# Second mixer of a two-layer encoder: two gated projections placed between pairs of the attention, scores as two products over 64 rows, one gate by exp

## The chip, the cores and the metric

The kernel runs on one core of a Trainium2 chip. Its time is the device time of one execution in microseconds (us); lower is better. TensorE (PE) multiplies matrices, VectorE (DVE) and ScalarE (ACT) work elementwise, GpSimd (POOL) helps and issues some of the DMAs, and SyncE (SP) issues the weight loads.

## The reference

512 tokens (two sequences of 256) of width 1024 pass through two layers; each is a mixer, a layernorm, a convolutional feed-forward part (FFN) and another layernorm. The first layer's mixer is a neighbourhood attention and is left as it was. The change is in the second layer's mixer:

```python
def odd_mixer(x, cos, sin, w_in, q_norm_g, w_uq, kv_norm_g, w_ukv,
              conv_w, conv_b, conv_ln_g, conv_ln_b, w_out):
    h = x @ w_in
    c_q, c_kv, k_r, glu_a, glu_g = split(h)            # 256, 128, 32, 512, 512 columns
    c = latent_attention(c_q, c_kv, k_r, ...)
    d = glu_a * jax.nn.sigmoid(glu_g)
    d = jax.nn.silu(layernorm(dwconv(d, conv_w, conv_b), conv_ln_g, conv_ln_b))
    return jnp.concatenate([c, d], axis=-1) @ w_out

def latent_attention(c_q, c_kv, k_rope_in, ...):       # 8 heads
    q_nope, q_rope = split(rmsnorm(c_q) @ w_uq)        # 64 and 32 per head
    k_nope, v = split(rmsnorm(c_kv) @ w_ukv)           # 64 and 64 per head
    q_rope, k_rope = apply_rope(q_rope), apply_rope(k_rope_in)   # k_rope is shared by the heads
    s = (q_nope . k_nope + q_rope . k_rope) * 96 ** -0.5
    return softmax(s) @ v
```

The depthwise convolution `dwconv` has 31 taps over 512 channels.

## The kernel before

Everything stays on chip as features by tokens (128 partitions x 512 tokens). A float32 matrix is split into two parts, hi and lo (ACT makes `whi`, DVE `wlo`), and a product is three matmuls of 128x512. The scores and their product with V stay in plain float32, where the trace records each matmul twice: `s` x4 in a row of the trace are two products.

The second mixer works on these pieces:

- `glu(i)`, i = 0 to 3: the gated projection of 128 channels, 48 matmuls into two banks of PSUM (tile `glu`). ACT takes the sigmoid of the second bank (L541, tile `sig`), DVE multiplies it with the first (L545, tile `dpad`). The convolution of the channels follows: 20 taps on DVE into a PSUM bank (`cacc`, L706), 9 as products on ACT (`pr`, L710, a ring of two halves) that POOL adds up (`acc`, L711). At the end DVE adds both (L712). `accps` and `acc2` hold the two sums.
- `cproj`, `chain`: the projection to q, k and rope inputs, the rms norm, the rotation of the rope part of k, and transposes back (tiles `craw`, `cT`, `krT`).
- `kvproj`, `qproj`: V, the 64 nope rows of k and q, and the rotated rope part of q (`qr`: two multiplications by `ropeT` and one addition on DVE). Rope rows are brought by DMAs on ACT's queue (L646) to rows 64 to 95 of `kT` and `qT`, so that each head has its 96 rows together.
- `attend(p)`, p = 0 to 3: a pair of heads, for each of two sequences. `attention` (L478) computes the scores of both heads (one bank of pool pB each, which has two), then per head the row maximum on DVE (`nmx`), exp on ACT (`er`, L492), the reciprocal of its sum on DVE (`ri`), the scaling on ACT (L499), four transposes on PE (`pt`), a copy on ACT (`PTr`, L508), and one step later the product with V on PE (`pv`), whose two heads stand in columns 0 to 63 and 64 to 127 of the array.
- `OutProj` (`op`, `dn` banks): the output projection, which fills PE's time between the attention's steps as far as its inputs exist.
- `conv_ln`: after the convolution, transposes to tokens (`ct`), mean and variance on DVE, `rstd` on POOL, the normalization on DVE (`cnm`), transposes back (`cb`, each needs the `cnm` of all four token tiles), silu on ACT, split, and the rest of the output projection.
- `ToFeat` (the `sink`): the residual. POOL loads four `xres` tiles and two rows (`rowg`, `rowb`), and applies the previous layernorm's gain and offset to the tiles (L193, L196; two tiles at once, the other two later). The `rstd` of `conv_ln` stand in POOL's queue behind the first two tiles.

The code is written in program order, and a scheduler that simulates the engines decides in which order each engine gets its instructions; this order is fixed at compile time, and each engine keeps to it. Program order before: `glu(0)`, `cproj`, `chain`, `glu(1)`, `glu(2)`, `kvproj`, `qproj`, `glu(3)`, `op.open(0)`, `attend(0..3)`. Sigmoid and exp lie in different tables of ACT; `preload(AF.Exp)` after the fourth sigmoid loads the one for exp.

Of the kernel before, what the change touches and what calls it, by code (L numbers as in the profile page):

```python
# [8 lines left out]
F32 = mybir.dt.float32  # L9
# [41 lines left out]
def tile_encoder(ctx: ExitStack, tc: tile.TileContext, I, O):  # L51
# [278 lines left out]
    def even_mixer():  # L330
# [103 lines left out]
        for p in range(4):  # L434
            bias = biases[p]
            qb, ka, kb = qks[p % 2]
            near = slice(0, 64), slice(64, 128)
            for j in range(2):
                ps = bank(pA, "qk")
                hi, lo = wload(I["wqk"][:, 2 * p + j].rearrange("p k n -> p (k n)"), 1024)  # L440
                gemm_feat(ps, hi, lo, xT)
                for h in range(2):
                    a, b = near[h], near[1 - h]
                    if j == 0:
                        nc.scalar.copy(out=qb[a, h, :], in_=ps[a])
                        nc.vector.tensor_tensor(out=qb[b, h, :], in0=ps[a], in1=qb[a, h, :].bitcast(F32),
                                                op=ALU.subtract)
                    else:
                        nc.scalar.copy(out=ka[a, h, :], in_=ps[a])
                        nc.gpsimd.tensor_copy(out=ka[b, h, :], in_=ka[a, h, :].bitcast(F32))  # L450
                        nc.vector.tensor_tensor(out=kb[a, h, :], in0=ps[a], in1=ka[a, h, :].bitcast(F32),
                                                op=ALU.subtract)

            def score(out, h, qs, ks, qb=qb, ka=ka, kb=kb):
                mm(out, qb[:, h, qs], ka[:, h, ks], True, False)
                mm(out, qb[:, h, qs], kb[:, h, ks], False, True)
# [72 lines left out]
    def odd_mixer(xT):  # L529
# [3 lines left out]
        def glu(i, by_seq=False):  # L533
# [3 lines left out]
            for seqs in ((0,), (1,)) if by_seq else ((0, 1),):  # L537
                for ps, hi, lo in pss:
                    gemm_feat(ps, hi, lo, xT, seqs)
            sg = tmp([P, 512], s="sig")  # L540
            nc.scalar.activation(out=sg, in_=pss[1][0], func=AF.Sigmoid)  # L541
            if i == 3:
                preload(AF.Exp, sg[:, 0:1])
            d = dpad[i]
            nc.vector.tensor_tensor(out=d[:, :, 15:15 + S], in0=pss[0][0].rearrange("p (s t) -> p s t", s=2),  # L545
                                    in1=sg.rearrange("p (s t) -> p s t", s=2), op=ALU.mult)
# [32 lines left out]
        def chain():  # L579
            cT = G["cT"] = [act([P, 2, T], F32R, "cT") for _ in range(3)]  # L580
            krT = G["krT"] = tmp([P, T], s="krT")
            psc = G["psc"]
            craw = []
            for s in range(2):
# [3 lines left out]
                for q in range(2):  # L588
# [10 lines left out]
                    nc.vector.tensor_tensor(out=c[:, q, 384:416], in0=ra, in1=rb, op=ALU.add)  # L599
# [7 lines left out]
            for i in (2, 0, 1, 3):  # L607
                w = P if i < 3 else 32
                for t in range(NT):
                    nc.tensor.transpose(ct_ps[i][0:w, t * P:(t + 1) * P],  # L610
                                        craw[t // 2][:, t % 2, i * P:i * P + w], ident)
                if i == 3:
                    nc.scalar.copy(out=krT[64:96, :], in_=ct_ps[3][0:32, :])
# [7 lines left out]
        def qproj():  # L621
            cT = G["cT"]
            ropeT = act([P, 2, S], s="ropeT")
            after_mm(nc.gpsimd.dma_start(out=ropeT, in_=I["ropeT"]), G["start"])
            wq = G["wq"]
            qT = G["qT"] = [act([P, 2, T], s="qT") for _ in range(4)]
# [9 lines left out]
            for r in range(2):  # L636
                ab = []
                for j in range(2):
                    ps = qfeat(pB, 4 + 2 * j + r)
                    a = tmp([P, 2, S], s="qr")  # L640
                    nc.vector.tensor_tensor(out=a, in0=ps.rearrange("p (s t) -> p s t", s=2),
                                            in1=ropeT[:, j:j + 1, :].broadcast_to([P, 2, S]), op=ALU.mult)
                    ab.append(a)
                nc.vector.tensor_tensor(out=ab[0], in0=ab[0], in1=ab[1], op=ALU.add)
                for h in range(4):
                    nc.scalar.dma_start(out=qT[2 * r + h // 2][64:96, h % 2, :],  # L646
                                        in_=ab[0][32 * h:32 * h + 32].rearrange("p s t -> p (s t)"))
                for p in (2 * r, 2 * r + 1):
                    ps = qfeat(pC, p)
                    for h in range(2):  # L650
                        nc.scalar.activation(out=qT[p][0:64, h, :], in_=ps[h * 64:h * 64 + 64, :], func=AF.Copy,
                                             scale=96 ** -0.5)

        def kvproj():
            cT, krT = G["cT"], G["krT"]
            wkv = G["wkv"]
            V = G["V"] = [act([P, 2, 512], s="V1") for _ in range(2)]
# [4 lines left out]
            kT = G["kT"] = [act([P, 2, T], s="kT") for _ in range(4)]  # L662
            for i in range(4):
                nc.scalar.dma_start(out=kT[i][64:96, :, :], in_=krT[64:96, None, :].broadcast_to([32, 2, T]))
            for p in range(4):
# [5 lines left out]
                for h in range(2):  # L671
                    nc.scalar.copy(out=kT[p][0:64, h, :], in_=ps[h * 64:h * 64 + 64, :])

        def attend(p):
            if p == 0:
                G["ring"] = Ring(2, "er"), Ring(2, "PTr")
            er, PTr = G["ring"]
            qT, kT = G["qT"], G["kT"]
# [3 lines left out]
            attention(p, lambda out, h, qs, ks: mm(out, qT[p][0:96, h, qs], kT[p][0:96, h, ks], True, True),  # L682
                      G["V"], mixT[p], lambda ps, h, e: ps, er, PTr, True)
# [145 lines left out]
def layout(inp):  # L829
# [21 lines left out]
    a["wuq"] = np.concatenate([v.reshape(2, P, -1) for v in (wq[..., :64], wr, wr2)], axis=2).transpose(1, 0, 2)  # L851
# [35 lines left out]
    a["ropeT"] = np.tile(r.transpose(2, 1, 0) * np.float32(96 ** -0.5), (4, 1, 1)).astype(np.float32)  # L887
# [19 lines left out]
```

## Time and profile before

| | |
|---|---|
| time, 3 runs | median 1104.42 us, 1104.25 to 1105.01 |
| profiled execution | 1104.58 us, span 1102.8 us, mean granted clock of PE 0.989 |
| PE busy | 1085.3 us, 98% of the span |
| DVE, ACT, POOL busy | 661.1, 490.4, 224.8 us |
| transposes of `craw` (end of `chain`) | about 585 us of the span |
| first matmul of k, `glu(2)`, first scores | 598.7, 602.3, 636.9 us |
| first matmul of the FFN behind the mixer | 731.5 us |

Times within the profile are in us from the start of the span. PE is nearly always busy, so what counts is how much work PE has and where it waits or runs at a lower clock; the busy time of another engine counts only where PE waits for it. The second mixer is the one place with a long wait of PE in the middle of the kernel.

### The profile page before, as it was taken

How to read it: one execution, taken by the hardware profiler on the slowest of the kernel's cores; microseconds unless marked ns; L12 is line 12 of the kernel's file. 1: busy time of each engine (PE TensorE's matmuls, PEld its weight loads, DVE VectorE, ACT ScalarE, POOL GpSimd, SP SyncE). 2: the span in 40 equal slices, each digit the busy share in tenths (PEclk: the TensorE clock that was granted, in tenths of full speed). 3: DMA queues.
4: the chain of work that ended last, by engine and by line, in shares of the span. 5: the costliest groups of instructions: out<-in, count | busy, mean ns of one | idle time of the engine just before them, and what ended most of it. 6: DMA issues, size and time to landing. Idle time of an engine off the chain costs nothing.

```text
span 1102.8 us, 13652 instructions
## 1 busy us (share of the span) xinstructions
PE 1085.3 (98%) x5210; PEld 901.9 (82%) x5210; DVE 661.1 (60%) x982; ACT 490.4 (44%) x792; POOL 224.8 (20%) x222
## 2 busy tenths in 40 slices
PE   9999999999999999999999989999999999999996
PEld 7888778988888888888898857799888888888885
DVE  5388956766565656423379996467665656542227
ACT  5425644544444444321266799355444444431110
POOL 0581001200000000005465756130000000000273
PEclk9999999999999999999999969999999999999998
DMA  7833222533333333555233122244333333222601
GB/s 259 256 107 96 62 109 97 169 99 96 96 96 96 96 99 101 202 171 177 77 117 91 44 82 81 70 151 120 99 96 96 96 96 96 96 96 96 220 28 76
DMA packets 36193, 124.34 MB, mean 113 GB/s; under 512 B 4352, under 2 KB 5120, under 8 KB 36128
## 3 DMA queue, kind: packets, MB, share of 16 engines
q1 hardware_dynamic: 28224, 99.00, 29.0%
q0 software_dynamic: 6480, 22.66, 5.9%
q10 hardware_dynamic: 1424, 1.80, 0.6%
q8 instruction: 41, 0.67, 0.3%
q14 instruction: 24, 0.20, 0.1%
HBM read 114.01 MB, written 8.39 MB: 111 GB/s over the span
## 4 chain that ended last, share of the span: by engine, by line
PE 93%; DVE 2%; DMA 1%; POOL 1%; ACT 1%; issue 1%; POOLq 0%; DVEq 0%; ACTq 0%
PE up L96 44%; PE dn L96 29%; PE qk L96 4%; PE op L96 4%; PE glu L96 3%; PE v L96 2%; PE u L96 2%; PE s L96 1%; PE pv L96 1%; PE pt L506 1%; PE lnT L236 1%; DVE cacc L706 1%; DMA rowg<-in_rows 1%; POOL xres L196 0%; DMA xraw<-in_xT 0%
## 5 line engine op out<-in xcount | busy, mean ns | idle before, releaser
L96 PE MATMUL up<-xT,whi 128*128 128x512 f32 (+1 forms) x1536 | 440.1, 372 | 0.0
L112 DVE TENSOR_TENSOR wlo<-raw,whi 128x1024 fp32r<-128x1024 f32 (+1 forms) x174 | 232.7, 1339 | 288.7 <-ACT whi L110 287.1
L96 PEld LDWEIGHTS up<-xT,whi 128*128 128x128 f32 x1536 | 279.8, 188 | 49.9
L110 ACT CAST whi<-raw 128x1024 fp32r<-128x1024 f32 (+1 forms) x174 | 182.2, 1050 | 246.1 <-PE dn L96 131.3
L96 PE MATMUL up<-xT,wlo 128*128 128x512 f32 (+1 forms) x768 | 283.9, 372 | 0.0
L96 PE MATMUL dn<-whi,gT 128*128 128x512 f32 x704 | 217.5, 390 | 0.0
L96 PEld LDWEIGHTS up<-xT,wlo 128*128 128x128 f32 x768 | 144.2, 188 | 25.0
L96 PEld LDWEIGHTS dn<-whi,gT 128*128 128x128 f32 x704 | 132.0, 188 | 27.2
L96 PE MATMUL dn<-wlo,gT 128*128 128x512 f32 x352 | 137.0, 389 | 0.0
L185 POOL DMA_DIRECT2D xres<-xscr x12 | 6.4, 540 | 577.2 <-PE dn L96 574.7
L96 PEld LDWEIGHTS dn<-wlo,gT 128*128 128x128 f32 x352 | 66.1, 188 | 13.8
L116 ACT CAST gT<-cv 128x512 fp32r<-128x512 f32 x44 | 27.3, 621 | 111.8 <-DVE cv L768 111.8
L757 ACT ACTIVATE cv<-up,par 128x512 f32<-128x512 f32 x88 | 67.9, 772 | 0.0
L760 DVE SCALAR_TENSOR_TENSOR cv<-up,par,cv 128x510 f32<-128x510 f32 x88 | 65.7, 747 | 2.7
L758 DVE SCALAR_TENSOR_TENSOR cv<-up,par,cv 128x510 f32<-128x510 f32 x88 | 65.3, 742 | 0.0
L767 ACT ACTIVATE cv<-cv 128x512 f32<-128x512 f32 x44 | 27.8, 633 | 83.3 <-DVE cv L760 83.3
L706 DVE SCALAR_TENSOR_TENSOR cacc<-dpad,par,cacc 128x512 f32<-128x512 f32 x80 | 58.7, 750 | 1.1
L711 POOL TENSOR_TENSOR acc<-acc,pr 128x512 f32<-128x512 f32 x36 | 50.1, 1391 | 31.1 <-ACT pr L710 29.1
L117 DVE TENSOR_TENSOR gT<-cv,gT 128x512 fp32r<-128x512 f32 x44 | 30.4, 691 | 27.5 <-ACT gT L116 27.5
L96 PE MATMUL op<-whi,mixT 128*128 128x512 f32 x128 | 44.6, 404 | 0.0
L96 PE MATMUL dn<-whi,mixT 128*128 128x512 f32 x128 | 43.0, 394 | 0.0
L96 PE MATMUL glu<-xT,khi 128*128 128x512 f32 (+1 forms) x160 | 41.9, 348 | 0.0
(194 smaller groups left out, 1347.3 us busy)
## 6 DMA issues: line engine op xcount, KB each, us to landing
raw<-in_wup SPq DMA_DIRECT2D x88, 512.0 KB, 3.7
raw<-in_wdn SPq DMA_DIRECT2D x44, 512.0 KB, 3.5
raw<-in_wout SPq DMA_DIRECT2D x16, 512.0 KB, 3.8
xscr<-xres POOLq DMA_DIRECT2D x12, 512.0 KB, 4.2
xres<-xscr POOLq DMA_DIRECT2D x12, 512.0 KB, 4.5
raw<-in_wqk SPq DMA_DIRECT2D x8, 512.0 KB, 6.2
raw<-in_wglu SPq DMA_DIRECT2D x8, 512.0 KB, 4.0
raw<-in_wug SPq DMA_DIRECT2D x7, 512.0 KB, 3.9
```

Of the source, the lines that this page charges most:

```text
L96: last_mm[0] = nc.tensor.matmul(out=out, lhsT=lhsT, rhs=rhs, start=first, stop=last)
L110: nc.scalar.copy(out=hi[:, :n], in_=raw[:, :n])
L112: nc.vector.tensor_tensor(out=lo[:, :n], in0=raw[:, :n], in1=hi[:, :n].bitcast(F32), op=ALU.subtract)
L116: nc.scalar.copy(out=dst[:, 0, sl], in_=src)
L117: nc.vector.tensor_tensor(out=dst[:, 1, sl], in0=src, in1=dst[:, 0, sl].bitcast(F32), op=ALU.subtract)
L236: nc.tensor.transpose(self.banks[k // 2][:, (k % 2) * S + q * P:(k % 2) * S + q * P + P], x[:, k * P:(k + 1) * P], ident)
L706: nc.vector.scalar_tensor_tensor(out=a, in0=dpad[i][:, :, j:j + S], scalar=pc("cw", i * 32 + j), in1=a, op0=ALU.mult, op1=ALU.add)
L711: nc.gpsimd.tensor_tensor(out=a2, in0=a2, in1=pr, op=ALU.add)
L757: nc.scalar.activation(out=c, in_=pv, func=AF.Identity, scale=pc(fw, ch * 4 + 1), bias=pc(fw, ch * 4 + 3))
L758: nc.vector.scalar_tensor_tensor(out=c[:, :, 1:S], in0=pv[:, :, 0:S - 1], scalar=pc(fw, ch * 4), in1=c[:, :, 1:S], op0=ALU.mult, op1=ALU.add)
L760: nc.vector.scalar_tensor_tensor(out=c[:, :, 0:S - 1], in0=pv[:, :, 1:S], scalar=pc(fw, ch * 4 + 2), in1=c[:, :, 0:S - 1], op0=ALU.mult, o ...
L767: nc.scalar.activation(out=cg, in_=cg, func=AF.Silu)
```

## The change

Five edits to the second mixer; outside it the order of instructions stays.

1. Program order: `glu(2)` comes after `qproj`, `glu(3)` after `attend(1)`, `op.open(0)` after `attend(2)`. The sink is created at `attend(2)` and no longer at `attend(1)`.
2. The scores of a head are two products of 64 rows each instead of one of 96: nope rows `kn`, `qn` and rope rows `kr`, `qr`. The first head of a pair uses rows 0 to 63, the second rows 64 to 127. The two halves of the rotation of q are left side by side (the weights of q are interleaved on the host for this), and k's rotated rope part is repeated four times, so that the matmul does the rotation's addition. This removes the additions and the DMAs of rope rows, and the copies to `qT` and `kT` become one of 128 rows for two of 64.
3. The fourth gate is made from exp: ACT takes exp(-g) and adds 1, DVE takes the reciprocal and multiplies. Exp's table is loaded behind the third gate.
4. The gate's instructions have high priority in the scheduler.
5. `V` and `kn` lie in pool `wp` (12 tiles, which the weights use), no longer in `actp`.

```diff
-            def score(out, h, qs, ks, qb=qb, ka=ka, kb=kb):
...
-                for h in range(2):
-                    score(pss[h][:, qt, :], h, slice(s * S + qt * P, s * S + qt * P + P), slice(s * S, s * S + S))
+                score([pss[h][:, qt, :] for h in range(2)], slice(s * S + qt * P, s * S + qt * P + P),
+                      slice(s * S, s * S + S))
...
+            with tc.high_priority():
+                gate(i, pss[0][0], pss[1][0])
...
+            if i < 3:
+                nc.scalar.activation(out=sg, in_=pg, func=AF.Sigmoid)
+                nc.vector.tensor_tensor(out=out, in0=va, in1=vs, op=ALU.mult)
+            else:
+                nc.scalar.activation(out=sg, in_=pg, func=AF.Exp, scale=-1.0)
+                nc.scalar.activation(out=sg, in_=sg, func=AF.Copy, bias=1.0)
+                nc.vector.reciprocal(out=sg, in_=sg)
+                nc.vector.tensor_tensor(out=out, in0=va, in1=vs, op=ALU.mult)
+            if i == 2:
                 preload(AF.Exp, sg[:, 0:1])
...
+            for p in range(4):
+                ps = qfeat(pB, 4 + p)
+                nc.vector.tensor_tensor(out=qr[p // 2][:, p % 2, :].rearrange("p (s t) -> p s t", s=2),
+                                        in0=ps.rearrange("p (s t) -> p s t", s=2), in1=ropeT, op=ALU.mult)
+                ps = qfeat(pC, p)
+                nc.scalar.activation(out=qn[p // 2][:, p % 2, :], in_=ps, func=AF.Copy, scale=96 ** -0.5)
...
+            V = G["V"] = [wp.tile([P, 2, 512], F32, tag="w", name=nm("V1")) for _ in range(2)]
...
+            kn = G["kn"] = [wp.tile([P, 2, T], F32, tag="w", name=nm("kn")) for _ in range(2)]
...
+            def score(out, qs, ks):
+                for q_, k_, first in ((qn, kn, True), (qr, krT, False)):
+                    for h in range(2):
+                        rows = slice(h * 64, h * 64 + 64)
+                        mm(out[h], q_[rows, qs], k_[rows, ks], first, not first)
...
-            if p == 1:
+            if p == 2:
                 G["sink"] = ToFeat(xscr[1], 1, last_mm[0], "ln1_g1", "ln1_b1", xscr[2], EARLY)
...
         glu(1)
-        glu(2)
         kvproj()
         qproj()
+        glu(2)
+        attend(0)
+        attend(1)
         glu(3)
         op = OutProj("wout1", mixT, [0, 1, 2, 3], [4, 5, 6, 7])
+        attend(2)
         op.open(0)
-        for p in range(4):
-            attend(p)
+        attend(3)
```

On PE, where the attention starts, the order before was this (`s_5102` and `s_5103` are the banks of the two heads of the first pair and sequence, `x2` two matmuls in a row):

```order
L96 MATMUL s_5102<-kT_4903,qT_4937 128x256
L96 MATMUL s_5103<-kT_4903,qT_4937 128x256
L96 MATMUL s_5102<-kT_4903,qT_4937 128x256
L96 MATMUL s_5103<-kT_4903,qT_4937 128x256
L96 MATMUL s_5138<-kT_4903,qT_4937 128x256 x2
L506 MATMUL pt_5117<-ident,er_5093 128x128 x4
L96 MATMUL s_5139<-kT_4903,qT_4937 128x256 x2
```

The same place on PE now, ahead of the fourth projection (`s_5005` and `s_5006` are the banks of the two heads, `glu_5187` is the first bank of `glu(3)`):

```order
L96 MATMUL s_5005<-kn_4848,qn_4870 128x256
L96 MATMUL s_5005<-kr_4683,qr_4872 128x256
L96 MATMUL s_5005<-kn_4848,qn_4870 128x256
L96 MATMUL s_5005<-kr_4683,qr_4872 128x256
L96 MATMUL s_5006<-kn_4848,qn_4870 128x256
L96 MATMUL s_5006<-kr_4683,qr_4872 128x256
L96 MATMUL s_5006<-kn_4848,qn_4870 128x256
L96 MATMUL s_5006<-kr_4683,qr_4872 128x256
L96 MATMUL glu_5187<-xT_4252,khi_3989 128x512 x2
L96 MATMUL glu_5187<-xT_4252,klo_3991 128x512
```

A head has four matmuls where it had two; the scheduler puts the four of one head together, though the program text alternates between the heads, and 48 matmuls of `glu(3)` follow the first scores, with scores and transposes of the next sequence between them.

On POOL, the order before, from the convolution's last additions to the last affine step, was:

```order
L711 TENSOR_TENSOR acc_705_4425<-acc_705_4425,pr_4428 128x512 x18
L185 DMA xres_5183<-xscr 128x1024
...
L176 DMA rowg_5191<-in_rows 128x1024
L176 DMA rowb_5192<-in_rows 128x1024
L193 TENSOR_TENSOR xres_5183<-xres_5183,rowg_5191 128x1024
L193 TENSOR_TENSOR xres_5185<-xres_5185,rowg_5191 128x1024
L196 TENSOR_TENSOR xres_5183<-xres_5183,rowb_5192 128x1024
L196 TENSOR_TENSOR xres_5185<-xres_5185,rowb_5192 128x1024
L165 TENSOR_TENSOR rstd_5661<-rstd_5661,epsc 128x1
L165 TENSOR_TENSOR rstd_5675<-rstd_5675,epsc 128x1
```

The same stretch of POOL now:

```order
L720 TENSOR_TENSOR acc_705_4425<-acc_705_4425,pr_4428 128x512 x16
L185 DMA xres_5247<-xscr 128x1024
...
L176 DMA rowg_5255<-in_rows 128x1024
L176 DMA rowb_5256<-in_rows 128x1024
L720 TENSOR_TENSOR acc_705_4425<-acc_705_4425,pr_4428 128x512 x2
L193 TENSOR_TENSOR xres_5247<-xres_5247,rowg_5255 128x1024
L193 TENSOR_TENSOR xres_5249<-xres_5249,rowg_5255 128x1024
L196 TENSOR_TENSOR xres_5247<-xres_5247,rowb_5256 128x1024
L196 TENSOR_TENSOR xres_5249<-xres_5249,rowb_5256 128x1024
L165 TENSOR_TENSOR rstd_5666<-rstd_5666,epsc 128x1
L165 TENSOR_TENSOR rstd_5680<-rstd_5680,epsc 128x1
```

The loads of the residual and its rows stand in front of the last two additions instead of behind all 18; the rest keeps its order, so the first `rstd` still comes behind two tiles' affine steps.

On DVE, the stretch with the new reciprocal reads now (`sig_5237` is the fourth gate, `nmx` and `ri` belong to the heads, `cacc_4993` to the third convolution):

```order
L490 TENSOR_REDUCE nmx_5103<-s_5093 128x2
L555 RECIPROCAL sig_5237<-sig_5237 128x512
L715 SCALAR_TENSOR_TENSOR cacc_4993<-dpad_4418,par,cacc_4993 128x512
L496 RECIPROCAL ri_5108<-rs_5105 128x2
L490 TENSOR_REDUCE nmx_5118<-s_5094 128x2
L117 TENSOR_TENSOR mixT_5004<-pv_5085,mixT_5004 128x256
L556 TENSOR_TENSOR dpad_4421<-glu_5187,sig_5237 128x2x256
```

The gate's reciprocal stands ahead of a head's `ri` and of the next head's `nmx`, both of which ACT needs for its next step.

## Rows read from the trace of the kernel before

**Rows 1.** Windows: length, busy PE, PEld, DVE, ACT, POOL, PEclk, DMA share, GB/s.
```profile
646.00:657.00 11.00, 10.86 (x31) 5.84 (x29) 10.86 (x21) 10.67 (x30) 7.63 (x6) 0.50 0.01 2
657.00:679.00 22.00, 21.65 (x124) 15.40 (x121) 16.61 (x37) 19.11 (x61) 13.57 (x12) 0.94 0.38 144
679.00:703.00 24.00, 24.00 (x135) 18.82 (x136) 9.94 (x24) 16.60 (x39) 10.41 (x6) 1.00 0.00 1
```

**Rows 2.** Timeline of PE where the attention starts: start, us, what, [idle before].
```profile
636.86 1.89 PE L96 MATMUL s<-kT,qT 96*128 96x256 f32 x8
643.44 2.08 PE L96 MATMUL s<-kT,qT 96*128 96x256 f32 x4 [4.69 <-ACT er L492]
648.55 1.30 PE L506 MATMUL pt<-ident,er 128*128 128x128 f32 x4
...
657.38 0.90 PE L506 MATMUL pt<-ident,er 128*128 128x128 f32 x3
658.08 1.86 PE L96 MATMUL s<-kT,qT 96*128 96x256 f32 x4
```

**Rows 3.** Chain that ended last, 598 to 735: start, us, what.
```profile
598.66 0.96 PE k L96 x3
...
602.34 10.89 PE glu L96 x48
...
637.60 0.60 ACT sig L541
...
679.57 0.87 PE s L96 x4
...
683.57 0.44 PE pt L506 x4
...
686.10 0.33 PE cb L734 x3
686.42 1.01 PE pv L96 x8
...
691.54 0.70 PE cb L734 x5
...
731.53 3.47 PE up L96 x29
```

**Rows 4.** Groups by line and form, 598 to 735: busy us, mean ns, idle before.
```profile
L96 PE MATMUL s<-kT,qT 96*128 96x256 f32 x64 | 21.5, 471 | 4.8 <-ACT er L492 4.7
...
L710 ACT ACTIVATE pr<-dpad,par 128x512 f32<-128x512 f32 x27 | 18.8, 720 | 4.5 <-POOL acc L711 4.5
L492 ACT ACTIVATE er<-s,nmx 128x256 f32<-128x256 f32 x32 | 14.8, 468 | 1.0 <-DVE nmx L489 1.0
...
L651 ACT ACTIVATE qT<-q 64x512 f32<-64x512 f32 x8 | 4.8, 594 | 4.8 <-DMA qT<-qr 4.7
...
L644 DVE TENSOR_TENSOR qr<-qr,qr 128x512 f32<-128x512 f32 x2 | 2.7, 1357 | 0.0
...
L495 DVE RECIPROCAL ri<-rs 128x2 f32<-128x2 f32 x16 | 2.5, 158 | 2.3 <-ACT er L492 2.1
...
L545 DVE TENSOR_TENSOR dpad<-glu,sig 128x512 f32<-128x512 f32 x3 | 2.1, 688 | 0.8 <-ACT sig L541 0.8
...
L164 DVE TENSOR_SCALAR rstd<-mv 128x1 f32<-128x1 f32 x4 | 0.6, 152 | 0.1
```

**Rows 5.** Timeline of POOL from the convolution's last addition on.
```profile
653.96 1.27 POOL L711 TENSOR_TENSOR acc<-acc,pr 128x512 f32<-128x512 f32 x1 [0.79 <-ACT pr L710]
657.76 2.12 POOL L185 DMA_DIRECT2D xres<-xscr  x4 [2.53 <-PE pv L96]
659.87 0.53 POOL L176 DMA_DIRECT2D rowg<-in_rows  x1
...
668.14 4.70 POOL L193 TENSOR_TENSOR xres<-xres,rowg 128x1024 f32<-128x1024 f32 x2 [7.22 <-DMA rowg<-in_rows]
672.80 4.67 POOL L196 TENSOR_TENSOR xres<-xres,rowb 128x1024 f32<-128x1024 f32 x2
677.44 1.10 POOL L165 TENSOR_TENSOR rstd<-rstd,epsc 128x1 f32<-128x1 f32 x2
...
682.17 4.72 POOL L193 TENSOR_TENSOR xres<-xres,rowg 128x1024 f32<-128x1024 f32 x2
```

More of the change, by code (lines that the diff above doesn't have):

```diff
@@ L580, in chain @@
             cT = G["cT"] = [act([P, 2, T], F32R, "cT") for _ in range(3)]
-            krT = G["krT"] = tmp([P, T], s="krT")
+            G["kr"] = act([P, 2, T], s="kr")
+            krT, ropeT = G["kr"][:, 0, :], G["kr"][:, 1, 0:S]
+            after_mm(nc.gpsimd.dma_start(out=ropeT, in_=I["ropeT"]), G["start"])
             psc = G["psc"]
@@ L607, in chain @@
             for i in (2, 0, 1, 3):
-                w = P if i < 3 else 32
                 for t in range(NT):
-                    nc.tensor.transpose(ct_ps[i][0:w, t * P:(t + 1) * P],
-                                        craw[t // 2][:, t % 2, i * P:i * P + w], ident)
+                    nc.tensor.transpose(ct_ps[i][:, t * P:(t + 1) * P],
+                                        craw[t // 2][:, t % 2, i * P:(i + 1) * P], ident)
                 if i == 3:
-                    nc.scalar.copy(out=krT[64:96, :], in_=ct_ps[3][0:32, :])
+                    nc.scalar.copy(out=krT, in_=ct_ps[3])
                 else:
@@ L622, in qproj @@
             cT = G["cT"]
-            ropeT = act([P, 2, S], s="ropeT")
-            after_mm(nc.gpsimd.dma_start(out=ropeT, in_=I["ropeT"]), G["start"])
             wq = G["wq"]
-            qT = G["qT"] = [act([P, 2, T], s="qT") for _ in range(4)]
+            ropeT = G["kr"][:, 1:2, 0:S].broadcast_to([P, 2, S])
+            qn = G["qn"] = [act([P, 2, T], s="qn") for _ in range(2)]
+            qr = G["qr"] = [act([P, 2, T], s="qr") for _ in range(2)]
             def qfeat(pool, c):
@@ L635, in qfeat @@
                 return ps
[L636 to L652, printed above, removed]
+            for p in range(4):
[4 more added lines that the diff above has]
+                nc.scalar.activation(out=qn[p // 2][:, p % 2, :], in_=ps, func=AF.Copy, scale=96 ** -0.5)
         def kvproj():
-            cT, krT = G["cT"], G["krT"]
+            cT = G["cT"]
             wkv = G["wkv"]
-            V = G["V"] = [act([P, 2, 512], s="V1") for _ in range(2)]
+            V = G["V"] = [wp.tile([P, 2, 512], F32, tag="w", name=nm("V1")) for _ in range(2)]
             for t in range(NT):
@@ L670, in kvproj @@
                 mm(ps, wl, cT[2][:, 0, :], False, True)
-                for h in range(2):
-                    nc.scalar.copy(out=kT[p][0:64, h, :], in_=ps[h * 64:h * 64 + 64, :])
+                nc.scalar.copy(out=kn[p // 2][:, p % 2, :], in_=ps)
         def attend(p):
@@ L677, in attend @@
             er, PTr = G["ring"]
-            qT, kT = G["qT"], G["kT"]
+            qn, kn, qr = (G[n][p // 2][:, p % 2, :] for n in ("qn", "kn", "qr"))
+            krT = G["kr"][:, 0, :]
+            def score(out, qs, ks):
+                for q_, k_, first in ((qn, kn, True), (qr, krT, False)):
+                    for h in range(2):
+                        rows = slice(h * 64, h * 64 + 64)
+                        mm(out[h], q_[rows, qs], k_[rows, ks], first, not first)
             mixT[p] = act([P, 2, T], F32R, "mixT")
-            if p == 1:
+            if p == 2:
                 G["sink"] = ToFeat(xscr[1], 1, last_mm[0], "ln1_g1", "ln1_b1", xscr[2], EARLY)
-            attention(p, lambda out, h, qs, ks: mm(out, qT[p][0:96, h, qs], kT[p][0:96, h, ks], True, True),
-                      G["V"], mixT[p], lambda ps, h, e: ps, er, PTr, True)
+            attention(p, score, G["V"], mixT[p], lambda ps, h, e: ps, er, PTr, True)
         mixT = [None] * 8
```

26 lines of the change are left out of this document (13 added, 13 removed).

## The prediction, made before the changed kernel was run

> **What bounds the kernel now.** The page comes first: PE is busy for 98% of the span, so the kernel is as long as PE's work and what PE loses between. The waits of PE name one long loss, 4.69 us in front of a score at 643.44 [rows 2]. There both heads' first scores are done (x8 at 636.86), and the two banks for scores come free only when ACT has taken the exps, which stand behind the fourth sigmoid of 637.60 [rows 3] and the table load behind it. The windows show the second loss: from 646 to 657 the granted clock is 0.50, the lower level of 1.2 GHz, and a mean of 0.94 over the next 22 us [rows 1]. 6% of 22 us below full are 2.6 us at half, so PE ran at half clock from 643.4 to about 659.6, 16.2 us, after its idle time. The same instructions show the price: four score matmuls take 2.08 us there [rows 2] and 0.87 at full clock [rows 3], four transposes 1.30 against 0.44 [rows 2, 3]. At half speed 16.2 us of work lose 8.1 us. Hole and clock together: 12.8 us. That is what a better order could give back. I argue in times of the span; the profiled execution took 1104.58 us, 0.16 above the median of the runs.
>
> **PE's side of the change.** Removed: the hole, if the scores of the first sequence lie ahead of `glu(3)`. Its 48 matmuls are 10.89 us of work [rows 3] that no exp holds up, so ACT's table load and first exps lie beside it. The order shows them there. I take the whole 12.8 us as gained.
>
> Added: a score of 96 rows becomes two of 64. The group of scores has 64 records for 32 products [rows 4], so four records, 0.87 us, are two products: 0.435 each [rows 3]. Do 64 rows cost less than 96? Four transposes of 128 rows by 128 columns take 0.44 us [rows 3], 0.11 for 128 columns; a score record of 96 rows and 256 columns takes 0.87 / 4 = 0.22, the same per column. So the rows do not set the price, and 64 products cost 27.8 us instead of 13.9: **+13.9 us**, unless the two heads run side by side. That they can is shown by `pv`, whose two heads lie in different columns: 8 records of 256 columns take 1.01 us [rows 3], which is 4 x 0.22 = 0.87 and 0.14 more, not 8 x 0.22. But `pv` alternates between its halves, and the new order of scores does not: four matmuls of the first head, then four of the second. Neighbours in different halves remain at five places, worth 5 x 0.22 = **-1.1 us**.
>
> The Trainium skill bears on this. "TensorE: Matmul & The Clock Gate", part "Why this matters for your kernels", says that one matmul over few rows takes as long as one over 128 and that the gain is the running of several tiles at once; its Part 3 says that matmuls start and end in program order. The trace agrees for the first in the rows above. By "TensorEngine Tiling (Array Packing)", section Theoretical Speedup, up to 2x is to be had at 64 rows; by that the scores would cost nothing more. I treat that as a rival, since the order speaks against it.
>
> The 0.14 us that a `pv` group takes beyond its columns lie at its entry and exit, 0.07 each. Scores of 64 rows use another division of the array than projections and transposes do; I count 39 changes of division in the new order against 16. 23 x 0.07 = **+1.6 us**. "TensorEngine Tiling", Key Properties, says that a change of division drains the engine, which the 0.14 agrees with.
>
> Nothing else on PE changes in number or size: the transposes of `craw` grow from 32 to 128 columns out, with the same columns streamed. PE's sum is -12.8 + 13.9 - 1.1 + 1.6 = **+1.6 us**, without any new wait.
>
> **The other engines.** ACT loses eight copies of 64 rows to `qT` at 0.59 [rows 4] and as many to `kT`, for four and four of 128 rows; DVE loses two additions of 1.36 [rows 4]; the DMAs of rope rows and ACT's wait of 4.7 us for them [rows 4] go. All of this is work beside PE, before the first exp; with the hole counted above it earns nothing of its own. `V` and `kn` in `wp` hold 4 of 12 weight tiles during the attention, so three casts of output weights go behind it, where ACT is busy 16.6 of 24 us and DVE 9.9 [rows 1]: nothing, unless an `op` matmul comes to its weights first. Uncovered that is one cast, about 1 us each.
>
> **The fourth gate.** exp and the addition of 1 take one more ACT step, 0.6 us. The reciprocal of 128x512 has no row. From below: an elementwise step of that size, 0.69 (`dpad`) [rows 4]. From above: `ri` with two elements per row takes 158 ns, a step with one element 152 [rows 4]; if all the difference is the price of an element, 512 at 6 ns and 0.1 fixed make 3.2 us. A two-element row says little on the slope, so I take the middle, 2 us. It stands on DVE ahead of a head's `ri` and the next `nmx`, and ACT waits for both; but PE has the scores, transposes, `pv` and six `op` matmuls of other heads to do there, and ACT's `pr` steps wait for the gate itself. Price on the path: with the step on ACT, 2.6 us more for the convolution, counted next. By the iterative divide that "VectorE: DVE Perf Modes" describes (a repeat count of 8), an estimate is 512 x 8 cycles, some 4.3 us (at 0.96 GHz), 2.3 more than I take.
>
> **The POOL chain, a new wait.** `glu(3)` now ends later. From 598.66 to 636.86 PE did k, v, q, `glu(2)` and `glu(3)` [rows 2, 3]. Without `glu(3)` that ends at 636.86 - 10.89 = 626.0. Then 8 products of scores (3.5), `glu(3)` (10.9), 8 products more (3.5) and 8 transposes (0.9): 644.8, where before it was 636.9. Before, from the fourth sigmoid at 637.60 to the end of the last addition at 653.96 + 1.27 = 655.2 were 17.6 us [rows 3, 5]. Counted from 644.8 with 2.6 for the gate: 665.0 for the last addition, 2.6 less for the sixteenth, if ACT had no more between its `pr` than before. It has: up to the `pr` of the sixteenth stand six pairs of exps and five of scales, 0.9 a pair by [rows 4], with three copies, two casts and a weight cast. With these `pr` at 0.66 and laid end to end from 647, when the first of them has its maximum, they make 18.6 us and end at 665.6, and with POOL's addition the sixteenth is done at about 667 (from 662 to 669). POOL issues the loads behind it. From the first to `rowg` 2.1 us, its landing until L193 starts 8.3, L193 and L196 for two tiles 9.3 (668.14 to 677.44) [rows 5]: 686.7. Two `rstd` 1.1, L193 for the other two tiles 4.7 [rows 5], two `rstd` 1.1, a `cnm` 0.9: the third `cnm` is there at about 694.5, where before it was there by 686.10 [rows 3]. DVE's order also puts the first two `cnm` ahead of the last heads' `nmx`, so the attention's end hangs on the same `rstd`.
>
> PE reaches the first `cb` transpose that needs the third `cnm` at: the first FFN matmul (731.53 + 1.6 = 733.1) less what stands between, 156 matmuls of 0.227, 34 transposes of 0.11 and two `pv` of 1.0 [rows 3], 41.1 us: 692.0. So PE waits 2.5 us. Sum: +1.6 + 2.5 = +4.1, 1104.58 + 4.1 = 1108.7; the bounds of the sixteenth addition move the wait from 0 to 4.5, so 1106.2 to 1110.7.
>
> **The rivals.**
>
> 1. No new wait: the sixteenth addition comes by 664.5 or PE is itself later in the attention by small amounts that the wait then absorbs. PE's sum alone, +1.6: 1106.2; if some of PE's short gaps among the attention's steps close too, down to 1102. For it: ACT's waits in [rows 4] are small; against it: the 8 us by which `glu(3)` moves.
> 2. The heads run side by side, or 64 rows are cheaper than the row of 96 says. PE gets 13.9 - 1.1 = 12.8 us back, and its sum alone would be 1093.4. But the POOL chain moves earlier only by what the scores ahead of `glu(3)`'s end save, 3.5 us: third `cnm` at 691.0, first FFN matmul at 732.1, 1105.2; only if POOL's additions also keep up better does it fall to 1096. I put it at 1101. This is the faster side. It decides when four scores in a row take under about 0.7 us.
> 3. PE's clock falls again. Before, it fell after 4.69 us of idle time [rows 2] and cost 8.1. The waits of the new order (at `pt`, at `cb`) could do the same: 1108.7 + 8.1 = 1116.8. For it: 16 heads whose steps of scores, maximum, exp, scale, transpose follow one another with two banks. Against it: more fillers on PE between.
>
> **Chances.** The POOL chain, as summed: 0.40. No new wait: 0.24. Side by side: 0.14. Clock: 0.22. No change within what a measurement tells is 0.2%, 2.2 us, so 1102.2 to 1106.6. Faster: 0.10 of the second rival, 0.08 of the first and 0.01: 0.19. Within: 0.14 of the first, 0.04 of the second, 0.05 of the forecast: 0.23. Slower: 0.58. The range, 1101 to 1115, leaves out the low part of the second rival and the high part of the third. I round the forecast to 1108.5.
>
> **What would show it.** Right: no idle time of 4 us before a score and clock 1.0 from 640 to 660; four score records of one head in 0.87 us; `xres` loads issued at 665 to 669 and PE waiting for `cnm` before `cb`; first FFN matmul at 735 to 736. Wrong: score records of two heads that start together (rival 2); PEclk under 0.9 in a window behind 650 (rival 3); a reciprocal above 3.2 us, or PE waits at `pt` that add up to more than 3 us, which would shift the place of the loss.

## The result, and the profile after

The changed kernel takes 1114.99 us (median of 4 runs, 1113.97 to 1115.25), the kernel before beside it 1104.38: a ratio of 1.0093, with a 95% interval of 1.0076 to 1.0111. That is 10.6 us slower. The prediction said slower, 1108.5 in a range of 1101 to 1115. The measured time lies at the very edge of that range, 0.01 us inside it, with two of the four executions beyond it, and the loss is two and a half times the forecast one. The profiled execution took 1113.97 us, the fastest of the four, with a span 9.4 us longer than before; what the others lost on top of it no trace shows.

The windows of the changed kernel, over the same stretches as [rows 1], with the same columns:

```profile
646.00:657.00 11.00, 11.00 (x57) 7.72 (x56) 10.93 (x16) 8.47 (x22) 1.47 (x2) 1.00 0.00 1
657.00:679.00 22.00, 19.67 (x96) 13.22 (x96) 18.71 (x34) 19.38 (x55) 14.01 (x15) 0.98 0.40 144
679.00:703.00 24.00, 20.71 (x126) 14.51 (x123) 12.01 (x30) 15.03 (x39) 20.09 (x12) 0.95 0.08 23
```

From 646 to 657, where PE ran at a granted clock of 0.50 before, it now has no idle time and a clock of 1.00. The loss has moved behind this window: PE idles 2.3 and 3.3 us in the two later ones, which before were all but full. The waits of PE in the mixer, and the chain that ended last, name the places:

```profile
PE ct L731 <- DVE cnm L169: 3.1, 2, 2.4
PE s L96 <- ACT er L493: 1.9, 4, 0.8
PE pt L507 <- ACT er L500: 0.2, 1, 0.2
PE pv L96 <- ACT PTr L509: 0.2, 1, 0.2
```

```profile
644.99 1.92 PE s L96 x8
646.91 0.58 PE pt L507 x4
...
665.73 0.62 ACT pr L719
...
669.85 8.18 DMA rowg<-in_rows
...
687.44 0.55 POOL rstd L165
...
688.01 0.57 DVE cnm L169
...
689.42 0.73 DVE cnm L169
...
690.29 0.63 PE ct L731 x4
...
740.95 4.07 PE up L96 x34
```

The chain runs over ACT's steps for the heads and the convolution (`pr`), the loads that POOL issues, the landing of `rowg`, four affine steps and `rstd`, and comes back to PE at a `ct` transpose at 690.3. The first matmul of the FFN starts at 740.95, 9.4 us later than in [rows 3]; behind it the two kernels take the same time.

PE's timeline, first where the first pair's scores stand, then at the longest wait:

```profile
625.87 0.70 PE L96 MATMUL s<-kn,qn 64*128 64x256 f32 x2
...
626.84 0.70 PE L96 MATMUL s<-kn,qn 64*128 64x256 f32 x4
627.27 0.70 PE L96 MATMUL s<-kr,qr 64*128 64x256 f32 x4
...
628.76 0.74 PE L96 MATMUL glu<-xT,khi 128*128 128x512 f32 x2
...
688.88 0.66 PE L731 MATMUL ct<-ident,acc 128*128 128x128 f32 x4 [2.35 <-DVE cnm L169]
690.29 0.63 PE L731 MATMUL ct<-ident,acc 128*128 128x128 f32 x4 [0.75 <-DVE cnm L169]
```

The rows marked x4 at 626.84 and 627.27 hold records of both heads that start together. So where the second head's scores follow the first head's without a wait, two products of each run side by side, although the order of the program has all four of the first head ahead: these eight products take 2.89 us from 625.87 to 628.76, not twice 1.92.

POOL's part (timeline) answers to [rows 5]:

```profile
666.48 1.27 POOL L720 TENSOR_TENSOR acc<-acc,pr 128x512 f32<-128x512 f32 x1 [0.79 <-ACT pr L719]
667.69 2.17 POOL L185 DMA_DIRECT2D xres<-xscr  x4
...
678.16 4.66 POOL L193 TENSOR_TENSOR xres<-xres,rowg 128x1024 f32<-128x1024 f32 x2 [4.59 <-DMA rowg<-in_rows]
682.79 4.65 POOL L196 TENSOR_TENSOR xres<-xres,rowb 128x1024 f32<-128x1024 f32 x2
687.41 1.11 POOL L165 TENSOR_TENSOR rstd<-rstd,epsc 128x1 f32<-128x1 f32 x2
691.00 4.90 POOL L193 TENSOR_TENSOR xres<-xres,rowg 128x1024 f32<-128x1024 f32 x2 [2.48 <-PE ct L731]
695.85 1.07 POOL L165 TENSOR_TENSOR rstd<-rstd,epsc 128x1 f32<-128x1 f32 x2
```

On DVE the gate's reciprocal stands between two maxima, and it is long; the last row is the third and fourth `cnm` (timeline of DVE):

```profile
647.02 0.68 DVE L490 TENSOR_REDUCE nmx<-s 128x2 f32<-128x512 f32 x1
647.63 3.34 DVE L555 RECIPROCAL sig<-sig 128x512 f32<-128x512 f32 x1
...
651.47 0.15 DVE L496 RECIPROCAL ri<-rs 128x2 f32<-128x2 f32 x1
651.54 0.67 DVE L490 TENSOR_REDUCE nmx<-s 128x2 f32<-128x512 f32 x1
...
696.44 1.53 DVE L169 TENSOR_SCALAR cnm<-ct,mv,rstd 128x512 f32<-128x512 f32 x2 [2.42 <-POOL rstd L165]
```

The whole mixer from the first matmul of k to the first of the FFN can be split in one row of windows for each kernel (before, then after):

```profile
598.66:731.37 132.71, 127.54 (x601) 98.69 (x601) 98.66 (x181) 93.93 (x208) 64.15 (x52) 0.94 0.23 74
```

```profile
598.74:740.79 142.05, 136.42 (x664) 104.62 (x664) 103.52 (x181) 92.17 (x202) 64.37 (x51) 0.99 0.22 70
```

Before: 5.2 us idle, and a mean clock of 0.94 over 132.7 us, which costs 8.0; that leaves 119.5 us of work at full clock. After: 5.6 idle, 1.4 by the clock, 135.0 of work. So PE's work grew by 15.5, the old loss of 13.2 went, and 7.0 of new loss came: 15.5 - 13.2 + 7.0 = 9.3. The clock has two digits here, so that each term that rests on it is good to about 0.7 us.

### The profile page after: what moved, and what is told of

The parts are those of the page before. It is cut to its first block, busy times and chain, and to the rows that moved or that the text cites. A ratio compares the mean times of both kernels' runs of the same rounds, so it can differ in the third digit from the quotient of the medians.

```text
span 1112.2 us, 13733 instructions
## 1 busy us (share of the span) xinstructions
PE 1094.4 (98%) x5274; PEld 909.0 (82%) x5274; DVE 665.8 (60%) x981; ACT 486.8 (44%) x785; POOL 222.5 (20%) x222
## 4 chain that ended last, share of the span: by engine, by line
PE 94%; ACT 2%; POOL 1%; DMA 1%; DVE 1%; issue 1%; POOLq 0%; DVEq 0%; ACTq 0%
PE up L96 43%; PE dn L96 29%; PE glu L96 4%; PE qk L96 4%; PE op L96 4%; PE v L96 2%; PE u L96 2%; PE s L96 2%; PE pt L507 1%; PE q L96 1%; PE lnT L236 1%; PE pv L96 1%; DMA rowg<-in_rows 1%; ACT pr L719 0%; DMA xraw<-in_xT 0%
## 5 line engine op out<-in xcount | busy, mean ns | idle before, releaser
L110 ACT CAST whi<-raw 128x1024 fp32r<-128x1024 f32 (+1 forms) x174 | 182.3, 1050 | 248.1 <-PE dn L96 131.5
L96 PEld LDWEIGHTS dn<-wlo,gT 128*128 128x128 f32 x352 | 66.2, 188 | 13.7
```

Of the source, the lines that this page charges most:

```text
L96: last_mm[0] = nc.tensor.matmul(out=out, lhsT=lhsT, rhs=rhs, start=first, stop=last)
L110: nc.scalar.copy(out=hi[:, :n], in_=raw[:, :n])
```

## The experiments

All were timed against the kernel before in the same session, whose medians were 1104.5 to 1104.9 us.

**The two heads' scores issued alternately.**

```diff
+                if on_act and h == 0:
+                    chain_mm[0] = tr
...
-                    for h in range(2):
+                    for h in (1, 0) if qs.start % S == 0 else (0, 1):
...
-                        mm(out[h], q_[rows, qs], k_[rows, ks], first, not first)
+                        with tc.issue_after(chain_mm[0].ins) if chain_mm[0] is not None else nullcontext():
+                            mm(out[h], q_[rows, qs], k_[rows, ks], first, not first)
+                        chain_mm[0] = last_mm[0]
```

`tr` is the last transpose of a sequence's first head, so the edit also ties the next sequence's scores behind it.

> The matmuls of the two heads' scores are issued alternately, first half of the rows, then the other, in one piece behind the transposes of the previous sequence's first head. Theory A (what the changed kernel lost is mainly PE's own work: 64 products one after the other, and the changes of the array's division): eight products that took 3.8 to 4 us take about 2.1, so PE has 12 us less to do; the chain through the fourth gate, POOL's loads and the rstd moves by the 3.5 to 4 us that the scores ahead of the gate save, and with it the end: 1107 to 1110. If the POOL chain did not bind at all: 1102 to 1103. Theory B (the two heads do not run at the same time over different rows, or PE's work is hidden anyway): 1113 to 1116.

Measured: 1121.67 us, ratio 1.0151 (1.0136 to 1.0166), slower than the changed kernel and beyond the ranges of both theories. Yet the matmuls did what theory A wanted. PE's timeline of the first sequence, eight products:

```profile
625.76 0.70 PE L96 MATMUL s<-kn,qn 64*128 64x256 f32 x4
626.29 0.60 PE L96 MATMUL s<-kr,qr 64*128 64x256 f32 x4
626.72 0.60 PE L96 MATMUL s<-kn,qn 64*128 64x256 f32 x4
627.16 0.60 PE L96 MATMUL s<-kr,qr 64*128 64x256 f32 x4
627.68 0.74 PE L96 MATMUL glu<-xT,khi 128*128 128x512 f32 x2
```

Eight products take 1.92 us here; in the changed kernel's chain four products of one head take 1.92. The two heads run side by side when their matmuls alternate. The waits of PE say where this went, the longest first:

```profile
PE pt L508 <- ACT er L501: 5.5, 4, 2.3
PE dn L96 <- ACT er L494: 2.9, 2, 1.8
PE ct L736 <- DVE acc L726: 1.9, 1, 1.9
```

PE now waits 12.8 us in all, and from 646 to 680 its clock is 0.75. From k to the FFN there are 150.2 us, with 13.2 idle and 12 lost by a mean clock of 0.92; that leaves 125 us of work instead of 135. So PE's work was cut, and more than that came back as waits and lost clock. ACT waits 11.4 us for `nmx`, against 7.6 in the changed kernel. A likely reading, not tested by itself: a bundle of eight can go only when both heads' banks are free and, here, behind a transpose, so the next maxima come later.

**Scores over 96 rows in the new order** (edit 2 undone: `chain`, `qproj`, `kvproj`, `attend` as before, with V kept in `wp`).

```diff
-                for q_, k_, first in ((qn, kn, True), (qr, krT, False)):
...
+                for h in range(2):
+                    mm(out[h], qT[p][0:96, h, qs], kT[p][0:96, h, ks], True, True)
```

> The scores are made as before the change (one product over 96 rows, rope rows brought by DMA, rotation added on DVE, copies of 64 rows); order of the projections, the exp gate, the high priority, V in the pool of weights and the later residual stay as changed. Theory A (scores and divisions of the array are the loss): half the score work and only the changes of division of pv, PE 18 us less than in the changed kernel: 1101 to 1105, the POOL chain holding back some. Theory B (the later fourth projection and its POOL chain are the loss): 1109 to 1113, with PE waiting at ct or cb as in the changed kernel.

Measured: 1108.71 us, 1.0036 (1.0023 to 1.0049): between the two theories. PE waits at other places:

```profile
PE pt L507 <- ACT er L500: 4.8, 4, 2.0
PE up L96 <- DVE xT L246: 2.1, 1, 2.1
PE op L96 <- ACT mixT L116: 1.6, 1, 1.6
```

Undoing edit 2 gains 6.3 us in this order. PE has less to do, but 9.0 of 132.6 us it stands idle before the FFN, and then waits for the layernorm.

**The residual created early again.**

```diff
-            if p == 2:
+            if p == 1:
                 G["sink"] = ToFeat(xscr[1], 1, last_mm[0], "ln1_g1", "ln1_b1", xscr[2], EARLY)
```

> Only the residual's loads and rows are created at the second pair of heads, as before the change; all else as changed. POOL then has the loads behind 9 additions instead of 16, some 17 us earlier, and the first affine steps between the additions. Theory A (PE's own work is the loss, the POOL chain only adds its 3.1 us of waits at ct and the half clock behind it): 1110 to 1112. Theory B (the POOL chain is the whole loss): 1105 to 1108. If the affine steps delay the convolution's last additions by their 9.3 us, the wait only moves: 1114 to 1117.

Measured: 1115.59 us with a wide spread (1111.57 to 1120.76), 1.0098 (1.0063 to 1.0134): no different from the changed kernel. The waits at `ct` are gone, but PE waits 4.2 us for ACT at three scores, the longest 2.8, and its mean clock from 660 to 700 is 0.83, which costs 6.8 us. POOL does the affine steps among the convolution's additions, whose last six start at 671.8. By the median it is the third case of the expectation, the wait moved; but two of the five executions, 1111.6 and 1111.9, lie in theory A's range, so this run does not decide between them.

**The gate without the reciprocal** (left out: the gate multiplies by 1 + exp(-g), so the values differ).

```diff
-                nc.vector.reciprocal(out=sg, in_=sg)
```

> The fourth gate's reciprocal of 128x512 is left out, so the gate multiplies by 1 + exp(-g) instead of dividing by it; all else as changed. The step took 3.34 us in the changed kernel, ahead of the gate's product, which starts the convolution that POOL's loads queue behind. If the gate is on the chain: 2 to 3.3 us off, 1111.7 to 1113. If other engines hold the chain anyway (ACT with its steps between the products): less than 1 us off, 1114 to 1115.

Measured: 1107.33 us, 1.0025 (1.0014 to 1.0036). This takes 7.7 us off, more than twice the step's own 3.34 us and more than either theory allowed. PE waits 1.5 us in all, at a clock of 1.00 up to the FFN. POOL's timeline:

```profile
666.92 2.17 POOL L185 DMA_DIRECT2D xres<-xscr  x4
...
677.88 4.67 POOL L193 TENSOR_TENSOR xres<-xres,rowg 128x1024 f32<-128x1024 f32 x2 [7.76 <-DMA rowg<-in_rows]
682.50 1.11 POOL L165 TENSOR_TENSOR rstd<-rstd,epsc 128x1 f32<-128x1 f32 x2
683.59 5.72 POOL L196 TENSOR_TENSOR xres<-xres,rowb 128x1024 f32<-128x1024 f32 x2
```

The loads start 0.8 us earlier, and L193, which waits for `rowg`, only 0.3. But the convolution's last sum on DVE comes at 671.5 instead of 675.0, in the order now made both `rstd` stand between L193 and L196, and they are done 4.9 us earlier.

**The affine steps queued behind the first two rstd.**

```diff
+                if t == 1:
+                    with tc.issue_after(last_rstd[0].ins):
+                        sink.res.affine(EARLY)
...
-                G["sink"] = ToFeat(xscr[1], 1, last_mm[0], "ln1_g1", "ln1_b1", xscr[2], EARLY)
+                G["sink"] = ToFeat(xscr[1], 1, last_mm[0], "ln1_g1", "ln1_b1", xscr[2], ())
```

> The changed kernel with one thing moved: POOL's affine steps of the first two residual tiles are queued behind the first two rstd of conv_ln instead of ahead of them; PE's order is the same up to the second half of the ct transposes. Theory A (the chain rowg, L193, L196, rstd, cnm, ct, cb sets the end of the mixer): the first two cnm come at about 684 instead of 688 to 690, PE's 3.1 us of wait at ct go, the last two cnm come some 4 us earlier: 1109 to 1111. Theory B (the attention's own steps on ACT and DVE set the end, the POOL chain only runs beside): 1113.5 to 1115.

Measured: 1118.66 us, 1.0130 (1.0115 to 1.0146), beyond the ranges of both theories. The waits of PE:

```profile
PE up L96 <- DVE xT L248: 2.3, 1, 2.3
...
PE up L96 <- POOL xT L250: 1.4, 1, 1.4
PE up L96 <- DVE xT L250: 0.7, 1, 0.7
```

The 3.1 us at `ct` are gone, as theory A says, and PE is ready for the FFN at 738.3, 2.5 us earlier. There it waits 4.4 us for the next layernorm: in the order now made the last `lnT` transposes follow each other without matmuls of the output projection between them. Behind these waits the clock is 0.57 from 743 to 751, another 3.4 us. 4.4 + 3.4 - 2.5 = 5.3, about what the profiled execution took longer than the changed kernel's, 1119.20 against 1113.97. So the chain through `rstd` was the path to the mixer's end, and shortening it there gained 2.5 us, which the next place took back and more.

**The old program order with everything else changed.**

```diff
-        kvproj()
-        qproj()
-        glu(2)
-        attend(0)
-        attend(1)
-        glu(3)
+        glu(2)
+        kvproj()
+        qproj()
+        glu(3)
...
-        attend(2)
         op.open(0)
-        attend(3)
+        for p in range(4):
+            attend(p)
```

> The program order of before (third and fourth gated projection ahead of the attention); scores of two times 64 rows, exp gate, priorities, pools and the later residual as changed. Theory A (ACT's and DVE's steps set the pace of the attention, PE's extra score work lies in time that PE would wait): 1104 to 1108, PE's waits in the attention smaller than its added work. Theory B (PE's added work counts in full): the waits of before stay and 13 to 18 us come on top: 1116 to 1122.

Measured: 1125.47 us (1120.04 to 1125.95), 1.0182 (1.0158 to 1.0205), past theory A and 3.5 us above theory B's range. The profiled execution is the fastest of the four, so its trace shows less than the median loss. PE's timeline where the attention starts:

```profile
638.06 0.60 PE L96 MATMUL s<-kr,qr 64*128 64x256 f32 x4
644.70 1.22 PE L96 MATMUL s<-kn,qn 64*128 64x256 f32 x2 [6.04 <-ACT er L493]
```

The hole is 6.04 us, longer than the 4.69 of [rows 2], with the clock at 0.50 from 646 to 660. The gate's reciprocal lies in it: DVE works on it from 639.07 to 642.42, and the first maximum that the exps need starts at 642.91. The new order is worth some 10 us to the split scores with this reciprocal. The kernel with scores over 96 rows in the new order was 3.8 us slower than the one before, but that difference takes in the exp gate, the priorities, the pool and the later residual too.

**tanh for the gate, scores over 96 rows, affine steps behind the rstd.**

```diff
-                nc.scalar.activation(out=sg, in_=pg, func=AF.Exp, scale=-1.0)
-                nc.scalar.activation(out=sg, in_=sg, func=AF.Copy, bias=1.0)
-                nc.vector.reciprocal(out=sg, in_=sg)
+                nc.scalar.activation(out=sg, in_=pg, func=AF.Tanh, scale=0.5)
+                nc.scalar.activation(out=sg, in_=sg, func=AF.Copy, scale=0.5, bias=0.5)
```

> The changed order with scores over 96 rows as before; the fourth gate as 0.5 + 0.5 tanh(g/2), two ACT steps and no reciprocal on DVE; and the affine steps behind the first two rstd. With scores over 96 rows alone it was 1108.7. If reciprocal and POOL chain are what is left of the loss: 1100 to 1104, below the kernel before. If ACT's pace with the convolution's products between the heads' steps is what is left: 1106 to 1109.

Measured: 1108.09 us, 1.0042 (1.0026 to 1.0059): the second case. PE's waits agree with ACT's pace as far as they go: 3.7 us at `pt` for `er`, 2.9 at `op` for `mixT` and 1.5 at scores for `er`, and 2.1 at the FFN for DVE.

**The kernel before with tanh for the fourth gate** (the same edit in `glu`, exp's table loaded behind the third gate).

> The kernel before with the fourth gate as 0.5 + 0.5 tanh(g/2) and the exp table loaded behind the third gate; order of the program as before. The table load of 1.28 us leaves the place between the fourth gate and the first exps. If that place sets the hole of 4.69 us and the half clock behind it: the hole shrinks by 1.3 to 2 us, 1100 to 1103, or 1096 if the clock holds. If DVE, busy all through, sets it: 1104 to 1105.

Measured: 1104.58 us, 1.0001 (0.9991 to 1.0010). The timeline of PE:

```profile
636.82 1.89 PE L96 MATMUL s<-kT,qT 96*128 96x256 f32 x8
641.89 1.13 PE L96 MATMUL s<-kT,qT 96*128 96x256 f32 x4 [3.17 <-ACT er L492]
644.95 1.30 PE L506 MATMUL pt<-ident,er 128*128 128x128 f32 x4 [1.93 <-ACT er L499]
```

The scores go on 1.5 us earlier, and PE then waits 1.93 us at the transposes: 5.1 us of holes instead of 4.69. DVE is busy 30.7 of the 33 us up to 646, in the kernel before 31.95. The time is as the third expectation has it, 1104 to 1105; the table load held the scores up, but without it another wait takes the place.

**tanh in the changed kernel**, the same five lines as above and nothing else.

> The changed kernel with the fourth gate as 0.5 + 0.5 tanh(g/2): two ACT steps as with exp, no reciprocal on DVE, and the whole gate computed. Theory A (what the kernel without the reciprocal gained, 7.7 us, is the 3.3 us of DVE in front of the heads' maxima and the convolution, and the order of rstd and affine steps that follows): 1106 to 1109. Theory B (it gained from the data): 1113 to 1115.

Measured: 1107.14 us, 1.0022 (1.0013 to 1.0032), as theory A says. So the whole gate can be had at the price of the kernel without the reciprocal. Its window from k to the FFN:

```profile
598.74:734.70 135.96, 134.54 (x667) 104.18 (x666) 102.83 (x181) 91.43 (x201) 66.12 (x51) 1.00 0.23 74
```

1.4 us are idle, none is lost by the clock. In this trace PE is all but full, and the mixer is 3.2 us longer than before.

**tanh with scores over 96 rows.**

> Changed order, scores over 96 rows, gate by tanh, affine steps where the scheduler puts them. Scores over 96 rows with the reciprocal took 1108.7. If the reciprocal costs there as it does with the split scores: 1101 to 1104. If that version is held by ACT's pace in the attention and by the first FFN matmul that waits for the layernorm: 1106 to 1108.

Measured: 1107.57 us, 1.0027 (1.0015 to 1.0039), no different from tanh with the split scores, and in the range of the second case. PE's work is about 12 us less (122.4 busy of 131.5), and 9.1 us of idle time stand in its place, most of it at `pt` and `op` for ACT; behind it PE waits 2.1 us for the layernorm.

**tanh with alternating scores**, the edits of the first experiment and of tanh, but the scores are tied only to each other and not to the transposes; and the same with the residual created early.

> Gate by tanh and the two heads' score matmuls issued alternately (the first one of a sequence alone, the other seven behind the transposes). Theory A (without the reciprocal PE's work sets the attention's pace again): half of the score time goes, 8 to 12 us less than with tanh alone: 1096 to 1101. Theory B (ACT and DVE set the pace whatever PE's work is; both heads' banks must be free before the seven can go): no gain or a loss, 1107 to 1118, with PE waiting for er.

> The same as the alternating scores with tanh, with the residual created at the second pair of heads. Theory A: with PE's work halved the POOL chain is next, and the earlier loads take it off the path: 1093 to 1099. Theory B: 1105 to 1118, and the early affine steps change it by under 2 us either way.

Measured: 1120.81 us (1115.04 to 1121.97), 1.0134 (1.0107 to 1.0160), and 1113.26, 1.0076 (1.0061 to 1.0091). Theory A failed in both. The first lies 2.8 us above theory B's range, the second inside it. PE waits for ACT's `er` and `mixT` in both (in the first 7.9 us at one `dn` matmul). The early residual changes it by 7.6, more than theory B's 2. Without the reciprocal and without the tie to the transposes alternating costs 13.7 us against tanh alone, so neither of these explains what it costs.

None of the versions of the changed kernel beats the kernel before; the nearest of those that compute the whole gate is the one with tanh, 2.4 us behind it.

## Why the prediction was right, and where it was not

The direction and the kinds of loss were right: more work on PE than the hole gives back, and a new wait behind POOL's chain. That the time fell inside the range was luck. The range reached to 1115 for the sake of a falling clock, which cost 1.4 us here; the loss came from the terms of the sum. In the windows' terms it was 9.3 us where the prediction had 4.1: 1.1 more work, 4.5 more of new loss, 0.4 more gained. Another 1.2 us lie between the profiled executions and the medians. Two of the prediction's own signs of being wrong came, too: a reciprocal above 3.2 us, and scores of two heads that start together.

**The gain of 12.8 us.** Right in size: hole and half clock were 13.2 us in the window's own terms and are gone. The reason given for the hole was only half right: the fourth sigmoid and the table load stand in the path, but with the load taken away the time stayed (the kernel before with tanh). What else sets it was not separated; DVE, which makes the maxima, was busy nearly all through. The rows by which the prediction priced the half clock, 2.08 against 0.87 us for scores and 1.30 against 0.44 for transposes, are from two views that count the last matmul's end differently; in the timeline alone they are 2.08 against 1.03 (at 682.54) and 1.30 against 0.60 (at 683.41). The sum does not rest on them.

**PE's added work.** The sum had 13.9 - 1.1 + 1.6 = 14.4 us; 15.5 were measured. The undersized term is the change of the array's division: a head's four products take 1.92 us where 8 x 0.22 are 1.73, and the four transposes behind them 0.58 instead of 0.44 [rows 3]. One visit to the 64-row division costs 0.33, not 0.14; the trace has thirteen such visits by scores, 4.3 us where 1.6 stood. The other way went the places where the heads meet: two of the five save about 0.75 us each and one 0.43, two nothing because the second head waits for its exps; 1.9 together, not 1.1. These two corrections make the sum 16.3, as close to 15.5 as the clock's two digits tell. That rows do not set the price held. That the new order keeps the heads apart held only in part. Matmuls starting in program order, which the prediction took from the Trainium skill's "TensorE: Matmul & The Clock Gate", Part 3, is not what the rows at 626.84 show: the second head's first product starts with the first head's third, ahead of the first head's fourth.

**The POOL chain.** Right in its steps: sixteenth addition done at 667.7 for 667, L193 at 678.2 for 677.4, `rstd` at 687.4 for 686.7. What failed is the step "PE waits 2.5 us at the first `cb`". PE waited earlier, at the third and fourth tile's `ct`, which wait for the first two `cnm`: 3.1 us. Since the later tiles' statistics are made from those `ct`, the chain ran a second round, and the third `cnm` began at 696.4, where the prediction had it done at 694.5. With 1.9 us at scores and 1.4 by the clock the new loss was 7.0 us where 2.5 stood.

**The reciprocal** was mis-sized, and its price on the path more than its length. I took 2 us, between 0.69 and 3.2; it took 3.34 us, above even the upper bound. The estimate from the Trainium skill's "VectorE: DVE Perf Modes", 4.3 us, was 1.0 us too long. The price on the path was to be 2.6 us with the step on ACT; without the reciprocal, or with tanh, the kernel takes 7.7 to 7.9 us less. Part of this may be the order on POOL, where both `rstd` then come ahead of L196. Moving `rstd` ahead with the reciprocal in place brought PE to the FFN 2.5 us earlier, leaving the reciprocal out 6.1 us (734.69 against 740.79); how the rest divides is open. Without the reciprocal PE's sum alone is left: +2.4 us by the medians, where I had +1.6.

**The rivals.** "No new wait" is what the kernel with tanh shows, 1107.1 for 1106.2. "Side by side" is true of the chip, and of this order only where two heads meet; and where the order was changed for it, the time rose, which I had not foreseen: PE is not what paces the attention when its work is cut. "The clock falls again" came only in small part, 1.4 us, but more in the alternating version (12 us) and in the one with the early residual (6.8).

So of the loss of 10.6 us, 7.7 to 7.9 are shown to hang on the gate's reciprocal: two different edits that remove it agree. The other 2.4 us are, by the windows, PE's added score work less the hole that the new order fills; this is argued and not shown, since taking the added work away with tanh gained nothing. That the split of the scores costs 6.3 us with the reciprocal and nothing with tanh shows that the parts do not add.

## What to carry to other kernels

How much of two small matmuls runs side by side depends on how the order alternates between their halves (1.92 us for eight products alternating, 2.89 for four and four); read the order that the scheduler made, not the loop. Before cutting the work of the engine that is 98% busy, look what stands behind it: with 12 us less for PE the kernel with tanh was no faster, and waits for ACT's steps for each head stood in the place of the work. A single long step on an engine whose queue carries short steps that others wait for can cost more than its length, here 7.7 us for 3.34; look for an operation that avoids it (here tanh, without a further table load) before moving work around it.

## What was unexpected on the chip

- Eight plain float32 score products over 64 rows and 256 columns take 1.92 us when the halves alternate, against 1.92 for four of one half. With four of one half ahead of four of the other, the second half's matmuls begin while two products of the first are still to come: 2.89 us.
- A visit to the 64-row division between full-array work costs about 0.33 us: 0.19 on the scores, 0.14 on the transposes behind them.
- A reciprocal of 128x512 on DVE takes 3.34 us, 6.5 ns for each of 512 columns; a product of the same size 0.69 [rows 4].
- tanh between exps needed no table load: from 598 to 735 ACT loads a table twice in the kernel with tanh, as in the changed one and the one before.
